# Projections of a decoder step on Trainium2: loads and TensorE's work in a written order from the fifth weight step on

## The chip, the core and the metric

The kernel runs on one core of one Trainium2 chip. A core has a matrix engine (TensorE: PE for the products, PEld for the loads of its stationary operand), three engines for elementwise work (VectorE: DVE, ScalarE: ACT, GpSimd: POOL), and SyncE (SP), which here only issues DMAs. Each engine works through its own list of instructions in order; semaphores tie the lists together. The metric is the device time of one execution in microseconds.

## The reference, cut to what matters

One inference step of a two-layer trunk for 512 prompt rows and 8 x 8 sample rows, width 1024. Layer 0 is dilated sliding-window attention, layer 1 a state-space layer, and each is followed by a gated feed-forward net. The change is in the first part of layer 0:

```python
qkv = (h @ w_qkv).reshape(B, T, 3, N_DIL, N_HEAD_SLOTS, HEAD_DIM)
q = rope(rmsnorm(qkv[:, :, 0], q_gain), pos)
k = rope(rmsnorm(qkv[:, :, 1], k_gain), pos)
v = qkv[:, :, 2]
...
s = jnp.einsum('bqhd,bqkhd->bqhk', q_blk, kf) * (HEAD_DIM ** -0.5)
```

There are three window groups: g0 (128 keys, every row), g1 (512, every 4th) and g2 (2048, every 16th). The prompt attends to itself; the 8 samples attend to their caches of keys and values, which lie in memory.

## The kernel before

**The stages.** Projections (to about 333 us), attention (to about 442 us), then the output projection, feed-forward nets and the state-space layer, in which PE is all but always busy. The change touches the projections alone.

**Weight steps.** `w_qkv` is taken in nine chunks of 512 columns, in the order q2, k2, v2, q1, k1, q0, k0, v0, v1 (letter and group), and each chunk in four steps of 256 rows: 36 weight steps, counted here from 0 to 35 (`turn[0]` in the code). In a step a weight tile `raw` (512 KB) comes from memory by a DMA on SP, ACT rounds it to `whi`, DVE makes the rest `wlo` = raw - whi, and PE runs 28 matmuls of 128x512: for each of the four prompt tiles t = 0..3 two times three (`whi` with the rows' rounded part, `wlo` with it, `whi` with their rest), then four for the sample rows (`xsp`). `raw` has four buffers, `whi` and `wlo` two each. The sums of a chunk stand in five PSUM tiles `acc`.

**After a chunk.** ACT and DVE evict the five tiles as `a` (the sample tile t = 4 through L378) and sum squares (L577, L578); a short chain (L110 to L120) makes `rq`. `finish(t)` then rotates a tile on DVE: a product `u` (L589), a sum (L591), a scaling by `rq` (L592). `turned` transposes the tile on PE (L604), ACT copies it to `qT` or `kT`, and POOL writes new keys out. The list `late` hands out `finish`, the sample tile first, at the ends of the following chunk's steps by `LATE` and `LAST`: two at the first, then one each.

**Sample scores.** For g2, the keys of a sample are multiplied elementwise with its query on DVE. A product takes a tile of the cache `kc` and a tile of queries read from a scratch in memory (`qscr`, written by SP once q2 is rotated), 512 KB each; one multiplication (L409) and one reduction into `P` (L410). There are 32, four to a sample, and `Close2` then brings a sample's `P` onto PE, adds the new keys and DVE takes the maxima (L432). For g1 and g0, a `Score` loads cache tiles, PE transposes them (L516), ACT copies, PE makes the dots (L527, L532), DVE evicts them (L534). All cache and query tiles share six buffers `kst`; `Close2` and the dots share one PSUM tile, `Sd`.

**What sets the order.** A scheduler orders each engine's list when the program is built. `keep_in_program_order` keeps marked instructions of an engine in the order in which they were written, among themselves; the others may move. Before, PE's work is kept from `PINNED` = step 20 on; `slot()` is called after each prompt tile and after the sample rows (five to a step) and runs what `later(n, ...)` set n slots ahead. `PLAN` says in which step products and scores begin, at its end: their loads are issued there, and the DVE work is written right behind.

Of the kernel before, what the change touches and what calls it, by code (L numbers as in the profile page):

```python
# [30 lines left out]
NEG = -1e30  # L31
SCALE = HD ** -0.5
KST = 6
RV, RF = 0.0, 0.7
PINNED = 20
LATE, LAST = (2, 1, 1, 1), (2, 2, 1, 0)
PLAN = {5: (2,), 6: (2,), 7: (2,), 8: (2,), 9: (2,), 10: (2,), 11: (2,), 12: (2, 2), 13: (2,), 14: (2, 2), 15: (2,), 16: (2,), 18: (2,), 19: (2,), 20: (2,),
        21: (1, 2), 22: (1, 2), 23: (1, 2), 24: (1, 2), 25: (1, 2), 26: (1, 2), 27: (1, 2), 28: (1, 2), 29: (0, 2), 30: (0, 2), 31: (0, 2),
        32: (0, 0, 2, 2), 33: (0, 2), 34: (0, 0, 2)}


def dram(ap, off, dims):
    return bass.AP(tensor=ap.tensor, offset=ap.offset + off, ap=[list(d) for d in dims])
# [286 lines left out]
                self.roots()  # L330


def qkv_chunk(nc, A, L, x, part, gi, step=None, rate=0.0, pre=None, slot=None):
    acc = L["acc"]
    c0 = (part * 3 + gi) * 512

    def mm(*a, **kw):
        ins = nc.tensor.matmul(*a, **kw)  # L338
        return ins if slot is None else L["tc"].keep_in_program_order(ins)

    ps = [acc.tile([128, 512], F32, name="acc") for _ in range(5)]
    for kk in range(4):
        raw = x.w[kk] if c0 == 1024 else L["fetch_w"](A["w_qkv"], 4608, kk * 2, 2, c0, 512, rate)
        if pre is not None and kk == 0:
            with L["tc"].issue_after(x.gmc.ins):
                wh, wl = L["split_w"](raw)
        elif pre is not None:
            with L["tc"].issue_after(x.mark[kk - 1].ins):
                wh, wl = L["split_w"](raw)
            x.lo = L["mark"][0]  # L350
# [19 lines left out]
        if step is not None:  # L370
            step()
    return ps


# [19 lines left out]
UNITS = (1, 4, 8)  # L394


def cache_tile(nc, A, pool_, name, gi, b, c0, n, kv):
    t = pool_.tile([128, 2, 512], F32, name=name)[:, :n]
    st = STRIDE[gi]
    nc.sync.dma_start(t, dram(A[CACHES[gi]], (b * WIN[gi] + c0) * 1024 + kv * 512, [[st * 1024, 128], [1024, n], [1, 512]]))  # L400
    return t


def products(nc, A, L, eng, kst, P, b, part):
    c0 = 2 * part
    kc = cache_tile(nc, A, kst, "kc", 2, b, c0, 2, 0)
    qb = kst.tile([128, 2, 512], F32, name="kc")
    nc.sync.dma_start(qb, dram(L["qscr"], (b * 8 + c0) * 512, [[0, 128], [512, 2], [1, 512]]))
    eng.tensor_tensor(kc, kc, qb, OP.mult)  # L409
    eng.tensor_reduce(P[:, :, 0:2, c0:c0 + 2].rearrange("p a h c -> p c a h"), kc.rearrange("p c (a h d) -> p c a h d", a=4, h=2), AX.X, OP.add)  # L410


class Close2:
# [9 lines left out]
    def turn(self, kept=True):  # L423
        nc, L, b = self.nc, self.L, self.b
        pin, kT, q0 = L["tc"].keep_in_program_order if kept else (lambda x: x), L["kT"][2], T + b * 8
        Sd = self.psp.tile([128, 136], F32, name=self.nm)
        ins = nc.tensor.transpose(Sd[:, 0:128], self.P.rearrange("p a b c -> p (a b c)"), L["ident"])
        pin(ins)
        for hp in range(4):
            pin(nc.tensor.matmul(Sd[hp * 32:hp * 32 + 32, 128:136], self.Q[:, hp, :], kT[:, hp, q0:q0 + 8], start=True, stop=True,  # L430
                                 tile_position=(0, hp * 32), skip_group_check=True))
        nc.vector.tensor_tensor_reduce(L["Sall"][:, b, 2, :], Sd, L["md"][:, 2, :], 1.0, -3e38, OP.add, OP.max, L["mx3"][:, b, 2:3])  # L432


def qkv_phase(nc, tc, A, es, L):
# [44 lines left out]
            queue.remove(x_)  # L480
            x_[1]()

    def score2(b, part):
        if part == 0:
            prods[b] = dk.tile([128, 4, 4, 8], F32, name="P2")
            g.memset(prods[b], 0.0)
        products(nc, A, L, v, kst, prods[b], b, part)
        if part == 3:
            c = Close2(nc, L, dk, psd, "Sd", prods.pop(b), b)
            if turn[0] < PINNED:  # L490
                c.turn(False)
            else:
                later(8, c.turn)

    class Score:
        def __init__(self, gi, b):
            self.gi, self.b, self.n = gi, b, UNITS[gi]
# [12 lines left out]
            self.kc = [cache_tile(nc, A, kst, "kc", gi, b, c0, min(2, n - c0), 0) for c0 in range(0, n, 2)]  # L510
            self.ks = {}

        def turn(self, u):
# [21 lines left out]

    fill = [[], [], []]
    turn = [0]
    zero = [0]

    def step():  # L540
        for _ in range((LATE if turn[0] < 28 else LAST)[turn[0] % 4]):
            if late:
                late.pop(0)()
        zero[0] = 0
        for gi in PLAN.get(turn[0], ()):
            x_ = fill[gi].pop(0)
            if gi == 2:
                score2(*x_)
                continue
            c = Score(gi, x_)  # L550
            if gi == 1:
                for u in range(4):
                    later(u + 3, lambda c=c, u=u: c.turn(u))
                    if u % 2:
                        later(u + 4, lambda c=c, u=u: c.dots((u - 1, u)))
            else:
                later(zero[0] + 2, lambda c=c: c.turn(0))
                later(zero[0] + 4, lambda c=c: c.dots((0,)))
                zero[0] += 1
        turn[0] += 1  # L560

    late = []

    def qk_chunk(gi, part):
        ps = qkv_chunk(nc, A, L, x, part, gi, step, 0.0, x.prep if gi == 2 and part == 0 else None, slot if turn[0] >= PINNED else None)
        sh = wk.tile([128, 5, 8], F32, name="sh")
        v.memset(sh[64:128, 4], 1.0)
        at = []
# [14 lines left out]
        def finish(t):  # L583
# [8 lines left out]
            v.tensor_tensor(a3[:pp], a3[:pp], rq[:pp, t, :, None].to_broadcast([pp, 8, 64]), OP.mult)  # L592
            if t == 4 and part == (gi < 2):
                fill[gi] += range(NB) if gi < 2 else [(b, p) for b in range(NB) for p in range(4)]
            if turn[0] < PINNED:
                turned(t, a, pp)
            else:
                later(4, lambda: turned(t, a, pp))

        def turned(t, a, pp):  # L600
            dst = (qT, kT)[part][gi]
            pt = ptp.tile([128, 4, 128], F32, name="pt")
            for hp in range(4):
                ins = te.transpose(pt[:, hp, :pp], a[:pp, hp * 128:(hp + 1) * 128], ident[:pp, :pp])  # L604
                if turn[0] >= PINNED:
                    tc.keep_in_program_order(ins)
            if gi == 0 and part == 1 and t < 4:
                s.activation(dst[:, :, t:T:4], pt, AF.Copy)
            else:
                s.activation(dst[:, :, t * 128:t * 128 + pp], pt[:, :, :pp], AF.Copy)  # L610
            if part == 1:
                kv_out(nc, A, gi, 0, t, a)
            elif gi == 2 and t == 4:
                nc.sync.dma_start(qscr, a[:64])

        late.extend((lambda t=t: finish(t)) for t in (4, 0, 1, 2, 3))

    def v_chunk(gi, wk, vt=None):
        ps = qkv_chunk(nc, A, L, x, 2, gi, step, RV, None, slot if turn[0] >= PINNED else None)
# [12 lines left out]
    qk_chunk(2, 0)  # L632
    qk_chunk(2, 1)
    v_chunk(2, wk, vt2)
    for gi in (1, 0):
        qk_chunk(gi, 0)
        qk_chunk(gi, 1)
    v_chunk(0, wk)
# [6 lines left out]
    nc.sync.dma_start(vt0, L["vtscr"].rearrange("t p c -> p t c"))  # L645
    nc.sync.dma_start(mp, A["c_mp"])
# [4 lines left out]
    assert not any(fill)  # L651
    return [vt0, vt1, vt2], mp


# [814 lines left out]
```

## Time and profile before

| what | value |
|---|---|
| median of 3 runs | 1537.76 us (1534.53 to 1542.42) |
| the profiled execution's own time | 1540.19 us |
| its span, first to last instruction | 1538.4 us |
| mean granted TensorE clock | 0.987 |
| PE busy | 1485.8 us, 97% of the span |
| DVE, ACT, POOL busy | 902.7, 521.2, 321.3 us |
| moved by DMA | 322.63 MB, mean 210 GB/s |

A row of a timeline holds the start in us from the span's beginning, the duration in us, engine, line, operation, what it writes and reads, and a count; in brackets, how long the engine stood idle before it and what ended that. SPq is the issue of a DMA on SP. A row of groups holds, after the bar, busy time in us and the mean duration in ns, then idle time before them and what ended it. A row of waits holds total, number and longest. A row of DMA issues holds the count, the size of one, and the median us to landing. A 389 ns matmul overlaps the next one, so PE's rate is read from start to start.

### The profile page before, as it was taken

The numbers are of one execution on the slowest core, as the hardware profiler recorded it, in microseconds if no ns is written. First come the engines' busy times: TensorE is split into PE (matmuls) and PEld (weight loads), VectorE is DVE, ScalarE is ACT, GpSimd is POOL, SyncE is SP. The second block draws the span as 40 slices with busy tenths as digits, with TensorE's granted clock in tenths as the row PEclk, the third lists the DMA queues.
The fourth block names the chain that finished last, engine by engine and source line by source line (L and its number), as shares of the span: only waits on it lengthen the run. The fifth ranks groups of instructions, "written<-read, shape, count | busy, mean of one in ns | idle before, by whom it ended". The sixth has DMA issues, their size and how long they took to land. (4 is left out here: it accounts for less than half of the span.)

```text
span 1538.4 us, 29552 instructions
## 1 busy us (share of the span) xinstructions
PE 1485.8 (97%) x12406; PEld 1391.0 (90%) x12406; DVE 902.7 (59%) x1507; ACT 521.2 (34%) x790; POOL 321.3 (21%) x368
## 2 busy tenths in 40 slices
PE   9999897898999999999999999999999999999998
PEld 7778675666799999999999999999999999999998
DVE  5899776444556954488789567853543333333342
ACT  4533444445544221222222353532332212221222
POOL 2012231220012107554344330030110001000100
PEclk9999999899999999999999999999999999999999
DMA  7599466788965655778766947965556555442222
GB/s 258 189 347 324 124 223 208 221 293 299 313 185 192 219 198 192 246 262 285 246 226 212 328 138 220 292 198 172 192 191 217 191 190 190 148 147 83 83 68 77
DMA packets 190493, 322.63 MB, mean 210 GB/s; under 512 B 39480, under 2 KB 137016, under 8 KB 188824
## 3 DMA queue, kind: packets, MB, share of 16 engines
q1 hardware_dynamic: 182888, 303.76, 58.9%
q10 hardware_dynamic: 4992, 10.04, 1.9%
q0 software_dynamic: 2480, 6.95, 1.2%
q8 instruction: 97, 1.59, 0.4%
q14 instruction: 36, 0.29, 0.1%
HBM read 289.22 MB, written 118.78 MB: 265 GB/s over the span
## 5 line engine op out<-in xcount | busy, mean ns | idle before, releaser
L101 DVE TENSOR_TENSOR wlo<-raw,whi 128x1024 fp32r<-128x1024 f32 x200 | 247.7, 1238 | 251.7 <-ACT whi L100 248.2
L100 ACT ACTIVATE whi<-raw 128x1024 fp32r<-128x1024 f32 x200 | 208.1, 1042 | 526.3 <-PE acc L107 407.6
L107 PE MATMUL acc<-xgl,whi 128*128 128x288 f32 x1760 | 379.0, 296 | 1.0 <-DVE xgl L172 1.0
L107 PE MATMUL acc<-xgh,wlo 128*128 128x288 f32 x1760 | 377.3, 295 | 0.0
L107 PE MATMUL acc<-xgh,whi 128*128 128x288 f32 x1760 | 377.1, 296 | 0.1
L107 PEld LDWEIGHTS acc<-xgl,whi 128*128 128x128 f32 x1760 | 282.6, 188 | 2.5 <-DVE xgl L172 1.3
L107 PEld LDWEIGHTS acc<-xgh,wlo 128*128 128x128 f32 x1760 | 282.9, 188 | 0.8 <-DVE wlo L101 0.4
L107 PEld LDWEIGHTS acc<-xgh,whi 128*128 128x128 f32 x1760 | 281.5, 188 | 0.7 <-DVE gt L906 0.3
L908 POOL TENSOR_TENSOR gt<-gt,rstd 128x576 f32<-128x576 f32 x44 | 77.2, 1756 | 430.4 <-ACT gt L907 430.3
L107 PE MATMUL acc<-hh,whi 128*128 128x288 f32 x704 | 151.3, 296 | 0.0
L107 PE MATMUL acc<-hh,wlo 128*128 128x288 f32 x704 | 151.1, 295 | 0.0
L107 PE MATMUL acc<-hl,whi 128*128 128x288 f32 x704 | 150.9, 295 | 0.0
L338 PE MATMUL acc<-wlo,xh 128*128 128x512 f32 x288 | 114.5, 399 | 2.8 <-DVE wlo L101 2.8
L338 PE MATMUL acc<-whi,xh 128*128 128x512 f32 x288 | 113.4, 415 | 1.3 <-ACT xh L277 1.1
L107 PEld LDWEIGHTS acc<-hh,wlo 128*128 128x128 f32 x704 | 113.0, 188 | 0.2 <-issue 0.2
L107 PEld LDWEIGHTS acc<-hl,whi 128*128 128x128 f32 x704 | 112.9, 188 | 0.2 <-issue 0.2
L107 PEld LDWEIGHTS acc<-hh,whi 128*128 128x128 f32 x704 | 113.0, 188 | 0.0
L338 PE MATMUL acc<-whi,xl 128*128 128x512 f32 x288 | 112.6, 398 | 0.0
L192 POOL TENSOR_TENSOR ssum<-ssum,sq 128x576 f32<-128x576 f32 x21 | 35.8, 1703 | 235.9 <-ACT sq L191 235.9
L338 PEld LDWEIGHTS acc<-wlo,xh 128*128 128x128 f32 x288 | 55.6, 193 | 14.5 <-DVE wlo L101 4.3
L338 PEld LDWEIGHTS acc<-whi,xh 128*128 128x128 f32 x288 | 55.2, 193 | 12.9 <-ACT xh L277 1.7
L409 DVE TENSOR_TENSOR kc<-kc 128x1024 f32<-128x1024 f32 x32 | 39.0, 1219 | 45.9 <-DMA kc<-qscr 45.9
(361 smaller groups left out, 1951.5 us busy)
## 6 DMA issues: line engine op xcount, KB each, us to landing
o_kv_s<-cache_kv_w SPq DMA_DIRECT2D x64, 1020.0 KB, 7.3
kc<-cache_kv_w SPq DMA_DIRECT2D x96, 512.0 KB, 5.8
raw<-ffn_w_gate SPq DMA_DIRECT2D x44, 512.0 KB, 4.1
raw<-ffn_w_up SPq DMA_DIRECT2D x44, 512.0 KB, 3.8
raw<-ffn_w_down SPq DMA_DIRECT2D x40, 512.0 KB, 3.5
raw<-w_qkv SPq DMA_DIRECT2D x36, 512.0 KB, 5.5
kc<-qscr SPq DMA_DIRECT2D x32, 512.0 KB, 6.1
o_kv_s<-cache_kv_w SPq DMA_DIRECT2D x16, 1008.0 KB, 6.1
```

Source lines behind the costliest of these rows:

```text
L100: s.activation(hi, raw, AF.Copy)
L101: mark[0] = v.tensor_tensor(lo, raw, hi.bitcast(F32), OP.subtract)
L107: te.matmul(ps[:, c, :HN], w, x[:, c * HN:(c + 1) * HN], start=first and i == 0, stop=last and i == 2)
L192: g.tensor_tensor(self.ss, self.ss, sq, OP.add)
L338: ins = nc.tensor.matmul(*a, **kw)
L409: eng.tensor_tensor(kc, kc, qb, OP.mult)
L908: g.tensor_tensor(t, t, nin.r, OP.mult)
```

## The change

- The loads of `w_qkv` from step 4 on are kept in written order on SP; step j issues the one for step j + 2.
- PE's matmuls and transposes are kept in written order from step 4 on, not 20. Transposes of a finished tile always come four slots after its `finish`; `Close2` comes ten slots after its last product was written.
- A product's two loads are issued at the beginning of the step before (`PAIRS`), in kept order; its DVE work is written behind the step's `wlo`. DVE's own order is left to the scheduler. The numbers per step change: two each in steps 12 to 15, none in 16, two in 32.
- Cache tiles of the scores (`SCORES`) are loaded at the beginning of their step, in kept order.
- `qscr` is written by a DMA of POOL, straight after the rotation, not by SP behind the transposes. The loads of `vt0` and `mp` are issued in step 34.

What is computed, and with how many instructions, stays. The core of the diff (the tables, whose rows only place the work, are cut):

```diff
-PINNED = 20
+CHUNKS = ((0, 2), (1, 2), (2, 2), (0, 1), (1, 1), (0, 0), (1, 0), (2, 0), (2, 1))
-PLAN = {5: (2,), 6: (2,), ...
+PAIRS = {6: 1, 7: 1, 8: 1, ...
+SCORES = {21: (1,), 22: (1,), ...
...
     for kk in range(4):
-        raw = x.w[kk] if c0 == 1024 else L["fetch_w"](A["w_qkv"], 4608, kk * 2, 2, c0, 512, rate)
+        mult = begin()
+        raw = raws.pop(0)
...
             wh, wl = L["split_w"](raw)
+        mult()
...
+    def begin():
+        j = turn[0]
+        if 4 <= j + 2 < 36:
+            part, gi = CHUNKS[(j + 2) // 4]
+            raw = L["ring"].tile([128, 2, 512], F32, name="raw", bufs=4)
+            kept(nc.sync.dma_start(raw, dram(A["w_qkv"], ...)))
+            raws.append(raw)
+        due = [ready.pop(0) for _ in range(PAIRS.get(j, 0))]
+        for _ in range(PAIRS.get(j + 1, 0)):
+            b, part = fill[2].pop(0)
+            kc = cache_tile(nc, A, kst, "kc", 2, b, 2 * part, 2, 0, kept)
+            qb = kst.tile([128, 2, 512], F32, name="kc")
+            kept(nc.sync.dma_start(qb, dram(qscr, ...)))
+            ready.append((b, part, kc, qb))
+        for gi in SCORES.get(j, ()):
+            b, n = fill[gi].pop(0), UNITS[gi]
+            cached.append((gi, b, [cache_tile(nc, A, kst, "kc", gi, b, c0, min(2, n - c0), 0, kept) for c0 in range(0, n, 2)]))
+        if j in notes:
+            notes[j]()
+
+        def mult():
+            for b, part, kc, qb in due:
...
+                v.tensor_tensor(kc, kc, qb, OP.mult)
+                v.tensor_reduce(prods[b][...], kc.rearrange(...), AX.X, OP.add)
+                if part == 3:
+                    later(10, Close2(nc, L, dk, psd, "Sd", prods.pop(b), b).turn)
...
-            if turn[0] < PINNED:
-                turned(t, a, pp)
-            else:
-                later(4, lambda: turned(t, a, pp))
+            if (gi, part, t) == (2, 0, 4):
+                g.dma_start(qscr, a[:64])
+            later(4, lambda: turned(t, a, pp))
...
-                ins = te.transpose(pt[:, hp, :pp], a[:pp, hp * 128:(hp + 1) * 128], ident[:pp, :pp])
-                if turn[0] >= PINNED:
-                    tc.keep_in_program_order(ins)
+                kept(te.transpose(pt[:, hp, :pp], a[:pp, hp * 128:(hp + 1) * 128], ident[:pp, :pp]))
...
-            elif gi == 2 and t == 4:
-                nc.sync.dma_start(qscr, a[:64])
```

**PE, where the sample tile and the first prompt tile of k2 are transposed.** Before, on PE; `whi_1046` and `wlo_1047` are the weights of step 13, `whi_1086` those of step 14, `a_716` and `a_696` the two tiles:

```order
L338 MATMUL acc_984<-whi_1046,xsp_121 128x512
L338 MATMUL acc_984<-wlo_1047,xsp_121 128x512
L604 MATMUL pt_776<-ident_63,a_716 128x64 x4
L604 MATMUL pt_787<-ident_63,a_696 128x128 x4
L338 MATMUL acc_980<-whi_1086,xh_119 128x512
```

And changed; `whi_794` and `wlo_795` are the weights of step 9, `whi_856` those of step 10, `a_712` and `a_692` the same two tiles:

```order
L337 MATMUL acc_732<-wlo_795,xh_119 128x512
L337 MATMUL acc_732<-whi_794,xl_120 128x512
L614 MATMUL pt_828<-ident_63,a_712 128x64 x4
L614 MATMUL pt_835<-ident_63,a_692 128x128 x4
L337 MATMUL acc_733<-whi_794,xsp_121 128x512
L337 MATMUL acc_733<-wlo_795,xsp_121 128x512
L337 MATMUL acc_733<-whi_794,xsp_121 128x512
L337 MATMUL acc_733<-wlo_795,xsp_121 128x512
L337 MATMUL acc_729<-whi_856,xh_119 128x512
```

The transposes moved from the end of step 13 to the fourth slot of step 9, ahead of that step's sample matmuls. Those of q1 moved in the same way from step 20 to step 17; those of k1 stand in step 21 in both.

**DVE, from step 10's `wlo` to the scaling of k2's sample tile.** Before, on DVE; the weights of steps 10, 11 and 12 are `raw_864`, `raw_915` and `raw_985`, and `a_716` is scaled 13 rows below the last row here:

```order
L101 TENSOR_TENSOR wlo_867<-raw_864,whi_866 128x1024
L409 TENSOR_TENSOR kc_909<-kc_909,kc_911 128x1024
L410 TENSOR_REDUCE P2_856<-kc_858 128x2x4x2
L101 TENSOR_TENSOR wlo_918<-raw_915,whi_917 128x1024
L589 TENSOR_TENSOR u_783<-a_696,C1_168 128x1024
...
L410 TENSOR_REDUCE P2_856<-kc_960 128x2x4x2
L101 TENSOR_TENSOR wlo_988<-raw_985,whi_987 128x1024
```

And changed, with seven rows left out (four short ones of the chain to `rq`, a memset, and two sums of L602); `raw_734` is the weight tile of step 10, and that of step 11 comes eight rows behind the last row here:

```order
L101 TENSOR_TENSOR wlo_857<-raw_734,whi_856 128x1024
L110 RECIPROCAL rq_719<-sq_720 128x40
L503 TENSOR_REDUCE P2_860<-kc_790 128x2x4x2
L600 TENSOR_TENSOR u_784<-a_692,C1_168 128x1024
...
L502 TENSOR_TENSOR kc_852<-kc_852,kc_854 128x1024
...
L503 TENSOR_REDUCE P2_860<-kc_852 128x2x4x2
...
L502 TENSOR_TENSOR kc_912<-kc_912,kc_914 128x1024
L600 TENSOR_TENSOR u_846<-a_697,C1_168 128x1024
...
L503 TENSOR_REDUCE P2_860<-kc_912 128x2x4x2
L502 TENSOR_TENSOR kc_916<-kc_916,kc_918 128x1024
...
L503 TENSOR_REDUCE P2_860<-kc_916 128x2x4x2
L600 TENSOR_TENSOR u_906<-a_702,C1_168 128x1024
L603 TENSOR_TENSOR a_712<-a_712,rq_719 64x512
```

The weights of steps 11 and 12, which stood between the products, moved behind the scaling; three multiplications and four reductions of the products, and three `u`, stand between step 10's `wlo` and the scaling. The like stretch of step 17 (q1, from step 18's `wlo`) has two multiplications and two reductions, that of step 21 (k1, from step 22's) one and one, that of step 5 (q2, from step 6's) none.

**SP, around the first scores.** Before, on SP; `raw` is a weight tile (`raw_1606` of step 22), `kc` a tile of a cache, or of queries where `qscr` is read:

```order
L88 DMA raw_1606<-w_qkv 128x2x512
L88 DMA raw_1699<-w_qkv 128x2x512
L400 DMA kc_1693<-cache_kv_w2048 128x2x512
L408 DMA kc_1695<-qscr_91 128x1024
L88 DMA raw_1860<-w_qkv 128x2x512
```

And changed, from the beginning of step 22 (`raw_1620` is the weight tile of step 24) to that of step 23:

```order
L482 DMA raw_1620<-w_qkv 128x2x512
L400 DMA kc_1622<-cache_kv_w2048 128x2x512
L489 DMA kc_1624<-qscr_91 128x1024
L400 DMA kc_1626<-cache_kv_w512 128x2x512
L400 DMA kc_1628<-cache_kv_w512 128x2x512
L482 DMA raw_1717<-w_qkv 128x2x512
```

Weight tiles no longer run ahead of the products' tiles as their buffers allow; each step has its weight tile first, then the pair of the next step, then its score's.

More of the change, by code (lines that the diff above doesn't have):

```diff
@@ L330, in prep, with qkv_chunk @@
                 self.roots()
-def qkv_chunk(nc, A, L, x, part, gi, step=None, rate=0.0, pre=None, slot=None):
+def qkv_chunk(nc, L, x, raws, begin, step, pre=None, slot=None):
     acc = L["acc"]
-    c0 = (part * 3 + gi) * 512
     def mm(*a, **kw):
@@ L369, in qkv_chunk @@
             slot()
-        if step is not None:
-            step()
+        step()
     return ps
@@ L394, with cache_tile @@
 UNITS = (1, 4, 8)
-def cache_tile(nc, A, pool_, name, gi, b, c0, n, kv):
+def cache_tile(nc, A, pool_, name, gi, b, c0, n, kv, kept=lambda x: x):
     t = pool_.tile([128, 2, 512], F32, name=name)[:, :n]
     st = STRIDE[gi]
-    nc.sync.dma_start(t, dram(A[CACHES[gi]], (b * WIN[gi] + c0) * 1024 + kv * 512, [[st * 1024, 128], [1024, n], [1, 512]]))
+    kept(nc.sync.dma_start(t, dram(A[CACHES[gi]], (b * WIN[gi] + c0) * 1024 + kv * 512, [[st * 1024, 128], [1024, n], [1, 512]])))
     return t
[L404 to L410, printed above, removed]
 class Close2:
@@ L481, in slot @@
             x_[1]()
[L483 to L489, printed above, removed]
-            if turn[0] < PINNED:
-                c.turn(False)
-            else:
-                later(8, c.turn)
+    kept = tc.keep_in_program_order
+    raws, ready, cached = list(x.w), [], []
@@ new lines, in begin @@
+    def begin():
[3 more added lines that the diff above has]
+            raw = L["ring"].tile([128, 2, 512], F32, name="raw", bufs=4)
+            kept(nc.sync.dma_start(raw, dram(A["w_qkv"], (j + 2) % 4 * 256 * 4608 + (part * 3 + gi) * 512, [[4608, 128], [128 * 4608, 2], [1, 512]])))
+            raws.append(raw)
[4 more added lines that the diff above has]
+            qb = kst.tile([128, 2, 512], F32, name="kc")
+            kept(nc.sync.dma_start(qb, dram(qscr, (b * 8 + 2 * part) * 512, [[0, 128], [512, 2], [1, 512]])))
+            ready.append((b, part, kc, qb))
[6 more added lines that the diff above has]
+            for b, part, kc, qb in due:
+                if part == 0:
+                    prods[b] = dk.tile([128, 4, 4, 8], F32, name="P2")
+                    g.memset(prods[b], 0.0)
+                v.tensor_tensor(kc, kc, qb, OP.mult)
+                v.tensor_reduce(prods[b][:, :, 0:2, 2 * part:2 * part + 2].rearrange("p a h c -> p c a h"), kc.rearrange("p c (a h d) -> p c a h d", a=4, h=2),
+                                AX.X, OP.add)
+                if part == 3:
+                    later(10, Close2(nc, L, dk, psd, "Sd", prods.pop(b), b).turn)
+        return mult
@@ L537, in qkv_phase @@
     turn = [0]
-    zero = [0]
+    notes = {}
     def step():
@@ L543, in step @@
                 late.pop(0)()
[L544 to L551, printed above, removed]
+        zero = 0
+        while cached:
+            c = Score(*cached.pop(0))
+            if c.gi == 1:
                 for u in range(4):
@@ L556, in step @@
             else:
-                later(zero[0] + 2, lambda c=c: c.turn(0))
-                later(zero[0] + 4, lambda c=c: c.dots((0,)))
-                zero[0] += 1
+                later(zero + 2, lambda c=c: c.turn(0))
+                later(zero + 4, lambda c=c: c.dots((0,)))
+                zero += 1
         turn[0] += 1
@@ L564, in qk_chunk @@
     def qk_chunk(gi, part):
-        ps = qkv_chunk(nc, A, L, x, part, gi, step, 0.0, x.prep if gi == 2 and part == 0 else None, slot if turn[0] >= PINNED else None)
+        first = (part, gi) == CHUNKS[0]
+        ps = qkv_chunk(nc, L, x, raws, begin, step, x.prep if first else None, None if first else slot)
         sh = wk.tile([128, 5, 8], F32, name="sh")
@@ L612, in turned @@
                 kv_out(nc, A, gi, 0, t, a)
-            elif gi == 2 and t == 4:
-                nc.sync.dma_start(qscr, a[:64])
         late.extend((lambda t=t: finish(t)) for t in (4, 0, 1, 2, 3))
     def v_chunk(gi, wk, vt=None):
-        ps = qkv_chunk(nc, A, L, x, 2, gi, step, RV, None, slot if turn[0] >= PINNED else None)
+        ps = qkv_chunk(nc, L, x, raws, begin, step, None, slot)
         for t in range(5):
@@ L630, in v_chunk @@
             kv_out(nc, A, gi, 1, t, a)
[L632 to L638, printed above, removed]
+    for part, gi in CHUNKS[:8]:
+        if part < 2:
+            qk_chunk(gi, part)
+        else:
+            v_chunk(gi, wk, vt2 if gi == 2 else None)
     assert not late
@@ L644, in qkv_phase, with values @@
     mp = vp.tile([128, 4, 512], BF16, name="mp")
-    nc.sync.dma_start(vt0, L["vtscr"].rearrange("t p c -> p t c"))
-    nc.sync.dma_start(mp, A["c_mp"])
+    def values():
+        nc.sync.dma_start(vt0, L["vtscr"].rearrange("t p c -> p t c"))
+        nc.sync.dma_start(mp, A["c_mp"])
+    notes[34] = values
     with ExitStack() as e4:
@@ L650, in qkv_phase @@
             slot()
-    assert not any(fill)
+    assert not any(fill) and not ready and not raws
     return [vt0, vt1, vt2], mp
```

19 lines of the change are left out of this document (8 added, 11 removed).

## The prediction

> **What bounds the kernel now.** I count the weight steps 0 to 35; step 4 is the fifth. First the windows by stage, for TensorE's (PE) idle time:
>
> ```profile
> 40.00:180.00 140.00, 131.04 (x613) 104.14 (x612) 130.20 (x176) 56.09 (x85) 27.41 (x45) 0.98 0.74 253
> 180.00:333.50 153.50, 137.25 (x1078) 106.34 (x1076) 86.62 (x133) 64.14 (x98) 35.85 (x95) 0.94 0.69 227
> 442.00:1538.40 1096.40, 1081.07 (x8440) 1071.80 (x8438) 610.93 (x934) 326.00 (x418) 245.55 (x203) 1.00 0.57 192
> ```
>
> After the first column pair come PE, weight loads, DVE, ACT, POOL, clock, DMA. The projections end near 333.5. PE idles 9.0 us from 40 to 180 and 16.2 us from 180 to there. DVE is busy 130.2 of 140 us in the first stretch: there it is nearly a second bound. What follows the projections keeps its work, so I carry the difference to the end one to one. PE's waits up to 345 us name the causes:
>
> ```profile
> PE Sd L427 <- DVE mx L534: 10.1, 3, 8.4
> PE acc L338 <- DVE a L378: 5.3, 1, 5.3
> PE pt L604 <- DVE a L592: 5.1, 4, 2.6
> PE acc L338 <- DVE wlo L101: 2.8, 4, 1.6
> ```
>
> All of them are for DVE. The two long ones, on DVE's and PE's timelines:
>
> ```profile
> 263.88 1.23 DVE L409 TENSOR_TENSOR kc<-kc 128x1024 f32<-128x1024 f32 x1 [3.15 <-DMA kc<-qscr]
> 267.96 0.29 DVE L534 CUSTOM_DVE_ANT_0 Sall<-Sd,md 128x136 f32<-128x136 f32 x1
> 301.06 1.23 DVE L409 TENSOR_TENSOR kc<-kc 128x1024 f32<-128x1024 f32 x1 [7.13 <-DMA kc<-qscr]
> 304.46 0.73 DVE L378 SCALAR_TENSOR_TENSOR a<-acc,rr,ks 64x512 f32<-64x512 f32 x1
> 305.34 0.76 PE L338 MATMUL acc<-whi,xsp 128*128 128x512 f32 x1 [5.29 <-DVE a L378]
> ```
>
> A product's multiplication stands in DVE's order and waits 3.15 and 7.13 us for its query tile; the eviction that PE needs is behind it. Finally the clock, in windows cut around the half-speed stretches:
>
> ```profile
> 166.70:170.10 3.40, 3.40 (x9) 2.66 (x9) 3.35 (x7) 1.63 (x3) 0.00 (x0) 0.50 0.00 0
> 176.90:180.30 3.40, 3.40 (x12) 2.72 (x11) 3.04 (x5) 1.65 (x2) 1.52 (x3) 0.50 0.60 215
> 268.30:272.50 4.20, 4.19 (x19) 2.95 (x19) 4.17 (x7) 0.60 (x1) 3.93 (x7) 0.50 0.67 183
> 305.40:310.00 4.60, 4.60 (x11) 3.63 (x12) 1.24 (x3) 1.06 (x1) 1.76 (x5) 0.50 0.96 294
> ```
>
> Each follows one of the waits. Busy at half speed for 15.6 us costs 7.8 us. So the whole prize is 9.0 + 16.2 + 7.8 = 33.0 us.
>
> **The weight loads in written order: nothing.**
>
> ```profile
> L100 ACT ACTIVATE whi<-raw 128x1024 fp32r<-128x1024 f32 x34 | 35.7, 1057 | 64.8 <-PE acc L338 59.5 <-DVE P L410 5.1
> raw<-w_qkv SPq DMA_DIRECT2D x36, 512.0 KB, 5.5
> DVE kc L409 <- DMA kc<-qscr: 45.9, 18, 7.1
> 312.32 0.38 SPq L645 DMA_DIRECT2D vt<-vtscr  x1
> ```
>
> ACT's rounding of a weight tile waits for PE, which still reads the tile two steps back (two buffers), and not for a landing. Weights are there already; earlier or tidier loads bring nothing. If that cover went, each late load would cost up to its 5.5 us to landing (second row) in that step. The loads of vt0 and mp, now tied to step 34, were issued at 312.3 before, about a step earlier and 21 us ahead of their use after 333.5: nothing either. The third row, DVE's 45.9 us for query tiles, is what the step's delay of the products is after; its part on PE's path is in the 33.0.
>
> **Products a step later, TensorE kept from step 4: removed, up to 33.0 us.** I credit all of it: the 8.4 and 5.3 lose their late tile, and what PE waited for before 180 (5.1 and 2.8) is priced anew below.
>
> **Added: pinned transposes of q2, k2, q1, k1.** A finished tile's transposes now stand four slots after its rotation was issued: steps 5, 9, 17 and 21 for the first two tiles of a chunk. Before, the scheduler set those of k2 in step 13 and of q1 in step 20. Only k1's, in step 21, were pinned there already, and this gives the price:
>
> ```profile
> 167.07 1.04 ACT L100 ACTIVATE whi<-raw 128x1024 fp32r<-128x1024 f32 x1
> 168.49 1.21 DVE L101 TENSOR_TENSOR wlo<-raw,whi 128x1024 fp32r<-128x1024 f32 x1
> 169.62 0.39 DVE L110 RECIPROCAL rq<-sq 128x40 f32<-128x40 f32 x1
> 175.21 1.88 DVE L592 TENSOR_TENSOR a<-a,rq 64x512 f32<-64x512 f32 x3
> 173.83 0.39 PE L338 MATMUL acc<-whi,xl 128*128 128x512 f32 x1
> 176.03 0.43 PE L604 MATMUL pt<-ident,a 64*128 64x64 f32 x4 [1.82 <-DVE a L592]
> ```
>
> PE ends step 20 at about 167; ACT may then round the weights of step 22, DVE subtracts, and DVE's order goes on from the reciprocal to the first L592 of three: 175.21 + 0.6 - 169.62 = 6.2 us. In the changed order the same list stands behind the same subtraction, with products set into it. Their prices, start to start:
>
> ```profile
> 73.32 1.22 DVE L410 TENSOR_REDUCE P<-kc 128x16 f32<-128x1024 f32 x1
> 74.45 1.21 DVE L409 TENSOR_TENSOR kc<-kc 128x1024 f32<-128x1024 f32 x1
> 75.58 0.68 DVE L578 TENSOR_REDUCE sh<-t 128x8 f32<-128x512 f32 x1
> 41.28 0.40 PE L338 MATMUL acc<-whi,xh 128*128 128x512 f32 x1
> 41.51 0.39 PE L338 MATMUL acc<-wlo,xh 128*128 128x512 f32 x1
> ```
>
> 1.13 us for a multiplication or a reduction; 0.23 us for a matmul, so PE is at its fourth slot after 24 x 0.23 = 5.5 us. From the step's start DVE needs at least 1.04 (rounding) + 1.13 (subtraction, 168.49 to 169.62) + 6.2 + 1.13 n, n being the products' instructions in the list. PE therefore waits at least 2.9 + 1.13 n. The orders give n = 0 in step 5, 7 in step 9 (three multiplications, four reductions), 4 in step 17 and 2 in step 21: 2.9 + 10.8 + 7.4 + 5.2 = 26.3 us. As a check on the trace, n = 0 gives 2.9 for step 21 as it was; PE came 1.7 us late through half clock, so 1.2, and it waited 1.8. Later pinned transposes (steps 25, 29) are where they were, and cost nothing after 180.
>
> Behind the waiting transposes stand the rest of the step and so the release of the weight buffers, which ACT and DVE wait for: the stall moves the whole chain, and no other engine makes it up, since DVE's own order holds the cause.
>
> **DVE's lateness on top: 8 us, bounds 0 and 12.** The queries' write to memory moves from SP to POOL's queue:
>
> ```profile
> 58.95 0.50 SPq L614 DMA_DIRECT2D qscr<-a  x1
> 61.56 0.34 SPq L408 DMA_DIRECT2D kc<-qscr  x1
> DMA to landing us min/median/max: 5.7/6.0/8.2
> ```
>
> From SP it was readable after 2.6 us; POOL's like write (to vscr, the third row; min, median, max) lands after 6.0. On POOL only set-up work stands ahead of it. That makes the first product some 3.4 us later, in a stretch where DVE has 10 us of idle time in 140, and the weight tiles of steps 8 and 9 stand behind it. The other 5 us are for DVE still at work when its weight tile is ready (above, it began 0.4 us late): about 1 us each in steps 5, 8, 9, 17, 21. If DVE's idle time takes it all in, 0; if the products' loads run late too, 12. [...]
>
> **Half clock after the four waits: 7.6 us, bounds 6.8 and 9.2.** By the four clock rows each costs 1.7 to 2.3 us.
>
> [...]
>
> **Close2 and dots in one slot: 6 us, bounds 1 and 10.** At the ends of steps 23 and 27 the closing matmuls now come due in the slot of a score's first dots, Close2 first, and both use the one PSUM tile Sd. PE waits for its eviction (0.29 us by the 267.96 row, with the handover 0.5). In DVE's order it stands behind a product whose tile comes free only as the score two steps back is turned. No trace shows it; I take 2 us each with some half clock, nearer the 1.82 than the 8.4.
>
> **Sum.** Added 26.3 + 8 + 7.6 + 6 = 47.9, less 33.0: +14.9 us. With all low bounds 34.1 - 33.0 = +1.1; with the high ones 57.5, and 6 us of the short waits left, +30.5. The profiled execution took 1540.19 us (span 1538.4), the runs' median is 1537.76, so about 1552 us as a median.
>
> **Rivals.**
> No change that can be measured (about 0.5%, 7.7 us): low bounds all round, 1539 us. For it: DVE has idle time later on; against: the chain leaves PE no slack in four places. 0.27.
> Faster: DVE clears the finish before PE gets there. It decides at 8.4 us from the step's start to the first L592; if the products in the list cost nothing there (n = 0), added is 4 x 2.9 + 6.8 + 1 = 19.4, net -13.6: 1524 us. For it: step 21 as it was; against: seven product instructions in DVE's order, which it can't pass. 0.10.
> SP's written order as a new bound: a load that waits for one of the six tiles holds the ones behind it, and the score tiles of steps 21 to 28 come late, say 2 us a step (a third of a 6.1 us load): 16 us more, 1568 us. For it:
>
> ```profile
> kc<-qscr SPq DMA_DIRECT2D x32, 512.0 KB, 6.1
> SPq L400 <- DMA kc<-qscr: 56.0, 13, 7.9
> ```
>
> SP waits much already; against: weights go first in each step, two steps ahead. 0.11.
> The change not doing what it says applies to the weight loads alone: they were early before.
>
> **Numbers.** The forecast itself (1546 to 1562) 0.52. Slower by over 0.5%: 0.52 + 0.11 = 0.63; within 0.27; faster 0.10. The range, 1533 to 1568, reaches over the low bounds and to the high ones.
>
> **What would show it.** Step 22 begins here before:
>
> ```profile
> 178.98 0.63 PE L338 MATMUL acc<-whi,xh 128*128 128x512 f32 x1
> ```
>
> PE's waits should name the transposes on L614 with DVE's a on L603: some 11 us or more in step 9, 7 in step 17, 5 in step 21; clock rows of 0.50 behind them. DVE's wait for query tiles should fall far below 45.9, and the 8.4 and 5.3 be gone. PE should reach step 22 near 205 to 212, and win back some 12 to 20 us by the end. If step 9's wait is under 3 us the forecast falls; if ACT's rounding waits for raw tiles, SP's rival stands.

## The result, and the profile after

The changed kernel takes 1554.73 us (median of 4 runs, 1553.58 to 1558.26) against 1536.14 us (1533.10 to 1542.42, 4 runs) of the kernel before: a ratio of 1.0125, 95% interval 1.0104 to 1.0145. It is slower, by 18.6 us, where 1552 was forecast. The profiled execution took 1555.63 us, its span 1553.9. Three single executions far from all others (2059 us of the kernel before, and 2898 and 2199 us in the experiments with the products behind the scaling and with later transposes) are left out of the medians here and below.

First where the time went. The windows are cut at the start of step 22 (179.0 us before, 205.7 after) and at the end of the projections (333.1 and 348.0); after the first column pair come PE, weight loads, DVE, ACT, POOL, clock, DMA. The kernel before:

```profile
40.00:179.00 139.00, 130.04 (x611) 103.33 (x610) 129.53 (x175) 55.24 (x85) 26.91 (x45) 0.98 0.74 252
179.00:333.10 154.10, 137.90 (x1068) 106.88 (x1070) 87.29 (x134) 64.59 (x99) 36.36 (x96) 0.94 0.69 227
333.10:1538.40 1205.30, 1181.09 (x10554) 1150.33 (x10552) 663.08 (x1136) 382.59 (x581) 249.40 (x207) 0.99 0.60 201
```

and the changed one:

```profile
40.00:205.70 165.70, 133.92 (x609) 108.07 (x610) 138.08 (x181) 56.74 (x84) 18.86 (x46) 0.89 0.66 234
205.70:348.00 142.30, 135.10 (x1077) 106.06 (x1079) 80.60 (x130) 64.63 (x99) 33.62 (x96) 0.97 0.66 228
348.00:1553.90 1205.90, 1182.56 (x10545) 1152.62 (x10545) 659.70 (x1134) 382.46 (x581) 250.33 (x208) 0.99 0.59 200
```

The first stretch is 26.7 us longer, the second 11.8 shorter, the third 0.6 longer: 15.5 in all. PE's idle time tells why. In the first stretch it grows from 9.0 us to 165.70 - 133.92 = 31.8, and the granted clock falls from 0.98 to 0.89. In the second it shrinks from 16.2 us to 7.2. What follows the projections keeps its time.

PE's waits up to 345 us in the changed kernel:

```profile
PE pt L614 <- DVE a L603: 26.2, 3, 11.6
PE Sd L541 <- DVE mx L423: 7.2, 2, 6.6
PE pt L614 <- issue: 3.3, 1, 3.3
PE acc L337 <- DVE a L378: 2.3, 2, 1.8
```

The first and the third row are the pinned transposes of steps 9, 17, 21 and of step 5. For step 5 the profile names nothing that ended the wait; on DVE's timeline the first scaling there starts at 56.56 and takes some 0.6 us, and PE goes on at 57.34. On PE's timeline, in that order of steps 5, 9, 17, 21 (the bracket is the idle time ahead of the row):

```profile
57.34 1.06 PE L614 MATMUL pt<-ident,a 64*128 64x64 f32 x5 [3.27 <-issue]
99.58 1.14 PE L614 MATMUL pt<-ident,a 64*128 64x64 f32 x5 [11.59 <-DVE a L603]
164.78 1.51 PE L614 MATMUL pt<-ident,a 64*128 64x64 f32 x7 [8.14 <-DVE a L603]
202.38 0.68 PE L614 MATMUL pt<-ident,a 64*128 64x64 f32 x4 [6.47 <-DVE a L603]
```

29.5 us in four places: nearly all of the first stretch's 31.8. And this is what DVE did meanwhile in step 9, from the weight subtraction to the scaling that the transposes need:

```profile
84.28 1.21 DVE L101 TENSOR_TENSOR wlo<-raw,whi 128x1024 fp32r<-128x1024 f32 x1
85.42 0.38 DVE L110 RECIPROCAL rq<-sq 128x40 f32<-128x40 f32 x1
85.73 1.15 DVE L503 TENSOR_REDUCE P<-kc 128x16 f32<-128x1024 f32 x1
...
96.59 1.21 DVE L503 TENSOR_REDUCE P<-kc 128x16 f32<-128x1024 f32 x1
97.72 1.21 DVE L600 TENSOR_TENSOR u<-a,C 128x1024 f32<-128x1024 f32 x1
98.85 1.88 DVE L603 TENSOR_TENSOR a<-a,rq 64x512 f32<-64x512 f32 x3
```

The list from the reciprocal to the end of the first scaling takes 98.85 + 0.6 - 85.42 = 14.0 us without a gap; 7 of its instructions are products. Behind each of the four waits, and behind the one of 6.57 us at the end of step 27, the clock is halved:

```profile
56.50:63.30 6.80, 5.96 (x19) 4.89 (x20) 6.21 (x9) 2.04 (x3) 2.07 (x3) 0.50 0.36 95
90.60:104.30 13.70, 4.71 (x16) 3.88 (x17) 13.70 (x19) 2.04 (x3) 1.75 (x3) 0.50 0.64 228
158.90:169.10 10.20, 4.32 (x15) 3.62 (x16) 9.75 (x15) 2.04 (x3) 3.12 (x6) 0.50 0.02 6
199.80:206.70 6.90, 4.32 (x15) 3.58 (x16) 6.83 (x12) 2.04 (x3) 2.27 (x4) 0.51 0.72 251
271.50:278.40 6.90, 4.78 (x28) 3.74 (x29) 6.35 (x11) 1.79 (x3) 0.00 (x0) 0.51 0.86 301
```

PE works 5.96 + 4.71 + 4.32 + 4.32 = 19.3 us at half speed behind the four waits, which costs 9.7 us, and 4.78 behind the fifth, which costs 2.4.

### The profile page after: what moved, and what is told of

The parts are those of the page before. It is cut to its first block, busy times and chain, and to the rows that moved or that the text cites. A ratio compares the mean times of both kernels' runs of the same rounds, so it can differ in the third digit from the quotient of the medians.

```text
span 1553.9 us, 29538 instructions
## 1 busy us (share of the span) xinstructions
PE 1488.2 (96%) x12406; PEld 1396.9 (90%) x12406; DVE 900.6 (58%) x1507; ACT 523.0 (34%) x790; POOL 311.2 (20%) x369
## 4 chain that ended last, share of the span: by engine, by line
PE 52%; DVE 2%; DMA 1%; ACT 0%; issue 0%; ACTq 0%; DVEq 0%
PE acc L107 48%; PE aux L107 1%; DMA u_scr<-uP 1%; PE acc L1261 1%; DVE cb L1171 1%; DVE kk L1180 0%; PE acc L1299 0%; PE acc L1300 0%; PE aux L1164 0%; PE aux L1300 0%; PE aux L1299 0%; PE aux L1175 0%; PE aux L937 0%; DVE Z L1281 0%; PE aux L1181 0%
## 5 line engine op out<-in xcount | busy, mean ns | idle before, releaser
L337 PE MATMUL acc<-whi,xh 128*128 128x512 f32 x288 | 118.5, 413 | 1.7 <-ACT xh L277 1.5
L337 PEld LDWEIGHTS acc<-whi,xl 128*128 128x128 f32 x288 | 55.0, 191 | 12.2
```

## Experiments

Three theories stood against each other. **A**: the transposes' places in PE's kept order cost, through DVE's list ahead of them. **B**: the products' delay and SP's written order cost. **C**: DVE simply has too much work, and whatever wait is taken away, another for DVE takes its place. Times are medians; before is measured beside them (1536.2 to 1536.8 us).

**One half of the change alone: TensorE kept from step 4.** On the kernel before:

```diff
-PINNED = 20
+PINNED = 4
```

> The kernel before with one number changed: TensorE's order is kept from step 4 in place of step 20; loads and products are as before. Theory A (the pinned transposes): DVE's list between the weight subtraction and the first scaled tile holds 0, 7, 2 and 0 product instructions in steps 5, 9, 17 and 21, so by 2.9 + 1.13 n PE waits 2.9 + 10.8 + 5.2 + 2.9 = 21.8 us, with some 7 us of half clock; against that stand about 9 us of idle time before 180 and 3.4 us of half clock that the kernel before has there. Step 22 starts at 192 to 202 (before 179.0), time 1550 to 1560. Theory B (the products' delay and SP's written order are what costs): nothing changes here, 1533 to 1542, step 22 near 179. Theory C (DVE's amount of work is the bound): work is the same as before, so within 5 us of 1537.

Measured: 1555.47 us (1553.47 to 1559.42), ratio 1.0133 (1.0105 to 1.0161). This one number costs as much as the whole change: 19.3 us. PE's two long waits of it:

```profile
103.21 1.14 PE L604 MATMUL pt<-ident,a 64*128 64x64 f32 x5 [15.13 <-DVE a L592]
169.58 1.73 PE L604 MATMUL pt<-ident,a 64*128 64x64 f32 x8 [8.77 <-DVE a L592]
```

They are longer than the 10.8 and 5.2 us that the formula gave, the one in step 21 shorter (0.9 against 2.9); step 22 starts at 203.0, just past A's 202. A stands, but its formula holds only where DVE comes to the whole list in time. Step 9 begins at 82.47 here and DVE's weight subtraction at 86.43, 4.0 us later, where the formula has 1.04; in step 21 the reciprocal (192.88) is done ahead of the subtraction (194.94), so that part of the list is no longer behind it. B is out as the only cause, and C too, since DVE's work is that of the kernel before.

**The other half: the change with TensorE kept only from step 20.**

```diff
+PINNED = 20
-    ps = qkv_chunk(nc, L, x, raws, begin, step, ..., None if first else slot)
+    ps = qkv_chunk(nc, L, x, raws, begin, step, ..., slot if turn[0] >= PINNED else None)
-            later(4, lambda: turned(t, a, pp))
+            if turn[0] < PINNED:
+                turned(t, a, pp)
+            else:
+                later(4, lambda: turned(t, a, pp))
```

(and the pins of the transposes and closing matmuls likewise)

> The changed kernel with TensorE's order kept only from step 20, as it was before; loads, the products' delay and the closing matmuls' ten slots stay. Theory A: the waits for the scaled tiles in steps 5, 9 and 17 (3.3, 11.6 and 8.1 us) and the half clock behind them (about 7.5 us) go; step 22 starts at 177 to 188, time 1525 to 1538. Theory B: the time stays at 1548 to 1557, step 22 at 200 or later, with waits for products or their tiles in place of the transposes. Theory C: DVE has 139 us of work ahead of step 22, so something of the gain stays out: step 22 at 188 to 196, 1538 to 1547.

Measured: 1530.14 us (1526.57 to 1534.83), ratio 0.9969 (0.9951 to 0.9987): faster than the kernel before by 6.0 us, and than the changed one by 24.6. Step 22 starts at 181.9. The delay and the loads are not what costs: B falls. C has this much right: at the seam of step 20, where the order begins to be kept, PE still waits for what DVE has left undone, as the timelines of PE and DVE show.

```profile
160.00 1.08 PE L622 MATMUL pt<-ident,a 128*128 128x128 f32 x4 [6.88 <-ACT t L378]
165.85 0.45 PE L622 MATMUL pt<-ident,a 128*128 128x128 f32 x1 [4.76 <-DVE a L608]
159.18 0.67 DVE L608 TENSOR_TENSOR a<-a,rq 128x512 f32<-128x512 f32 x1
```

The first row names ACT, but what PE turns there is a scaled tile, and DVE's scaling ended at 159.85, 0.15 us ahead of it.

**The dose: no products in DVE's list.** PE's order stays exactly as changed; a product's multiplication may only be issued behind the scaling of a chunk's first two tiles, which makes n = 0 in steps 9, 17 and 21 where it was 7, 4 and 2.

```diff
-                v.tensor_tensor(kc, kc, qb, OP.mult)
+                with tc.issue_after(scaled[0]):
+                    v.tensor_tensor(kc, kc, qb, OP.mult)
...
-            v.tensor_tensor(a3[:pp], a3[:pp], rq[:pp, t, :, None]...)
+            fs = v.tensor_tensor(a3[:pp], a3[:pp], rq[:pp, t, :, None]...)
+            if t in (4, 0):
+                scaled[:] = [fs.ins]
```

> The changed kernel with one rule more: a product's multiplication is issued on DVE behind the last written scaling of a chunk's first two tiles, so n is 0 in steps 5, 9, 17 and 21; PE's order and the transposes' places are untouched. Theory A: by 2.9 + 1.13 n each of the four waits is about 2.9 (together 11 to 14 us in place of 29.5), step 22 at 183 to 193, time 1530 to 1541. Theory B: the waits are for late products; pushing them back further costs, 1555 or more. Theory C: DVE's work is what is late; the 18 us come back as waits of PE for weight subtractions (a line L101) and the time is 1547 to 1556.

Measured: 1532.77 us (9 executions; interval of the ratio to before 0.9967 to 1.0002), 22.0 us under the changed kernel. The waits of steps 5, 9, 17 and 21:

```profile
57.66 0.43 PE L617 MATMUL pt<-ident,a 64*128 64x64 f32 x4 [3.29 <-issue]
88.77 0.46 PE L617 MATMUL pt<-ident,a 64*128 64x64 f32 x4 [1.39 <-DVE a L604]
145.06 1.15 PE L617 MATMUL pt<-ident,a 64*128 64x64 f32 x7 [1.19 <-DVE a L604]
175.38 0.46 PE L617 MATMUL pt<-ident,a 64*128 64x64 f32 x4 [1.69 <-DVE a L604]
```

Step 5, which had no products in its list, is as it was; the other three fall from 26.2 to 4.3 us. The only new rule is one on DVE's order, so the products in the list are shown to be the price. The 1.2 to 1.7 us are less than the 2.9 of the formula: without the products DVE does the reciprocal and the first product `u` of a rotation (in step 9 at 81.32 and 81.63) before it comes to the weight subtraction (83.06), and the whole of the list no longer stands behind it.

**The same cure from PE's side: transposes later.** PE's order is kept from step 4, DVE is left alone; the transposes come 5 or 10 slots later.

```diff
+WAITS = {(0, 2, 4): 9, (0, 2, 0): 9, (1, 2, 4): 14, (1, 2, 0): 14, ..., (0, 1, 4): 14, (0, 1, 0): 14, ...}
-            later(4, lambda: turned(t, a, pp))
+            later(WAITS.get((part, gi, t), 4), lambda: turned(t, a, pp))
-                    later(10, Close2(...).turn)
+                    later(16 if turn[0] < 12 else 10, Close2(...).turn)
```

> The changed kernel with PE's kept transposes moved back: those of q2 and k2 and of q1 and k1 by 5 or 10 slots for the first two tiles and 5 for some of the others, and the closing matmuls before step 12 by 6. PE's order is kept as before. Theory A: no PE wait for a scaled tile over 3 us in steps 5 to 21; 29.5 us of waiting and up to 9.6 us of half clock go, step 22 at 172 to 186, time 1518 to 1535. Theory B: the place of the transposes does not matter, 1548 to 1557. Theory C: PE waits for the weight subtractions instead (their own list now holds the products), step 22 at 190 or later, 1540 to 1550.

Measured: 1528.47 us (9 executions), ratio 0.9957 (0.9939 to 0.9975); step 22 starts at 181.3, and PE's waits for scaled tiles shrink to

```profile
PE pt L615 <- DVE a L604: 10.0, 4, 3.9
```

One of them is over the 3 us that A allowed; the time is in A's range and below C's.

**The weight loads alone**, on the kernel before:

```diff
-        raw = x.w[kk] if c0 == 1024 else L["fetch_w"](A["w_qkv"], ...)
+        ahead()      # kept load of the tile two steps on
+        raw = x.w.pop(0)
```

> The kernel before with its weight loads alone in a written order, two steps ahead; products and TensorE's order as before. If they cost and bring nothing, as the prediction had it: 1531 to 1541. If a good part of the 6 us by which the changed kernel with TensorE kept from step 20 beat the kernel before comes from these loads and not from the products' delay: 1528 to 1532. If SP's written order holds other loads up: over 1541.

Measured: 1536.35 us against 1536.81, ratio 0.9991 (0.9968 to 1.0013). Nothing beyond the interval, as priced.

**The shared slot.** The change set ten slots for the closing matmuls; the kernel before had eight (from step 20 on), and this run goes back to them.

```diff
-                    later(10, Close2(nc, L, dk, psd, "Sd", prods.pop(b), b).turn)
+                    later(8, Close2(nc, L, dk, psd, "Sd", prods.pop(b), b).turn)
```

> The changed kernel with the closing matmuls eight slots after the last product in place of ten, so that no score's first dots share their slot. If the shared slot is what costs: the waits of 6.6 and 0.6 us for the eviction of Sd and some 2.7 us of half clock go, 1543 to 1549; the prediction's own figure for this term was 6, so 1549. If DVE's wait for a query tile ahead of that eviction is what costs, wherever the closing matmuls stand: the wait moves to the closing matmuls themselves, 1552 to 1558.

Measured: 1548.48 us (ratio to before 1.0068, 1.0048 to 1.0088), 6.25 us under the changed kernel. DVE shows how. In the changed kernel at the end of step 27:

```profile
269.59 1.23 DVE L502 TENSOR_TENSOR kc<-kc 128x1024 f32<-128x1024 f32 x1 [6.56 <-DMA kc<-qscr]
270.85 1.22 DVE L503 TENSOR_REDUCE P<-kc 128x16 f32<-128x1024 f32 x1
271.99 1.27 DVE L589 TENSOR_REDUCE sh<-t 128x8 f32<-128x512 f32 x2
273.18 0.29 DVE L423 CUSTOM_DVE_ANT_0 Sall<-Sd,md 128x136 f32<-128x136 f32 x1
```

and with the closing matmuls two slots earlier:

```profile
263.82 0.30 DVE L423 CUSTOM_DVE_ANT_0 Sall<-Sd,md 128x136 f32<-128x136 f32 x1 [0.45 <-PE Sd L421]
269.53 1.23 DVE L502 TENSOR_TENSOR kc<-kc 128x1024 f32<-128x1024 f32 x1 [5.41 <-DMA kc<-qscr]
```

DVE waits for its tile all the same, 5.41 us in place of 6.56. But the eviction of Sd (L423) now stands ahead of that wait and not behind it, and of PE's 7.2 us for `Sd` 0.6 are left.

**The queries' write back on SP's queue.**

```diff
-                g.dma_start(qscr, a[:64])
+                nc.sync.dma_start(qscr, a[:64])
```

> The changed kernel with the queries written to memory from SP's queue again in place of POOL's. By the prediction's step the first product comes some 3.4 us earlier and up to that much is won: 1551 to 1555. If the 30.3 us that SP's queue stood behind that write in the changed kernel delay the weight tiles of steps 8 and 9 and with them the wait in step 9: 1543 to 1549. If neither is on PE's path: 1553 to 1557.

Measured: 1554.57 us (5 runs; ratio to before 1.0099, 1.0066 to 1.0132), the changed kernel's 1554.73 again. SP's queue stands still in both, in the changed kernel 30.3 us for the first product's read of the queries and here 35.5 us for the write itself. The changed kernel's row:

```profile
SPq L489 <- DMA qscr<-a: 30.3, 1, 30.3
```

Nothing that PE needs is late for it there: of ACT's waits for weight tiles in the changed kernel up to 360 us, two are for a load, and both end before 12 us.

```profile
ACT whi L100 <- PE acc L337: 29.3, 13, 5.8
ACT whi L100 <- DMA raw<-w_qkv: 4.8, 2, 4.3
```

But the run does not bring the first product 3.4 us forward: it starts at 66.88 here and at 64.25 in the changed kernel, and ACT waits 2.54 us for a weight tile here (until 61.91). What the write costs is read from the rows of the changed kernel:

```profile
57.55 0.77 POOL L607 DMA_DIRECT2D qscr<-a  x1 [32.24 <-DVE a L603]
60.05 0.34 SPq L489 DMA_DIRECT2D kc<-qscr  x1
```

From POOL's issue to the first read that had waited for it are 2.5 us; from SP it was 2.6 us before (58.95 to 61.56). The 3.4 us were never there.

**All three mendings at once**, the order kept from step 4 (products behind the scaling, transposes later, closing matmuls 14 slots after the last product before step 12 and 8 from there):

> The changed kernel, TensorE's order kept from step 4 as in it, with the products behind the scaling, the transposes later by the table of the run on it (closing matmuls at fourteen slots before step 12) and the closing matmuls eight slots after the last product from there. If the pinned transposes and the shared slot are all that a kept order costs: no PE wait over 2 us before 300, 1518 to 1526. If DVE's amount of work decides once they are gone: PE waits for weight subtractions, 1527 to 1535, no better than either mending alone.

Measured: 1523.48 us (1519.22 to 1528.71, 8 runs), ratio 0.9916 (0.9887 to 0.9944): faster than both kernels. The windows up to step 22 (171.8 here) and to the end of the projections:

```profile
40.00:171.80 131.80, 124.82 (x600) 100.55 (x600) 122.61 (x165) 54.14 (x82) 18.75 (x42) 1.00 0.69 251
171.80:314.10 142.30, 137.02 (x1085) 106.31 (x1086) 94.06 (x146) 66.19 (x101) 43.01 (x99) 0.98 0.80 267
```

DVE has 122.61 us of work ahead of step 22 where the changed kernel had 138.08: what need not be done there has moved behind it, where DVE has room (94.06 of 142.30). So C was no bound at these times either. A's "no wait over 2 us" was too strict: one of 2.6 us in step 12 and one of 3.95 in step 27 are left.

**The slot without the kept order, and with the dose.** The run with TensorE kept from step 20 and the one with the products behind the scaling, each with `later(8, ...)` for the closing matmuls:

> The changed kernel with TensorE's order kept only from step 20 and the closing matmuls eight slots after the last product. If the kept order and the shared slot are separate costs that add up: the 6.1 us by which the shared slot was dear with the order kept from step 4 go here too (PE waited 5.4 and 0.7 us there, with 3.4 us of half clock behind), 1522 to 1526. If the wait for Sd only moves to another place once PE is earlier: 1528 to 1533.

> The changed kernel, order kept from step 4, transposes in their places, with the products behind the scaling and the closing matmuls eight slots after the last product. If the two costs add up: 1533.7 less about 6, 1525 to 1530, and PE's waits in steps 9, 17 and 21 stay under 2 us. If the closing matmuls' own wait (5.0 us near the end of step 30 in the run with ten slots) only moves: 1531 to 1536.

Measured: 1523.71 us (ratio 0.9921, 0.9902 to 0.9940) and 1527.12 us (0.9956, 0.9932 to 0.9980). The two slots are worth 6.4 and 5.65 us here, and 6.25 in the changed kernel: a separate cost that adds up. The 5.65 is the coarsest of the three, since the six executions of that run go from 1523.55 to 1535.17 us. In it PE waits 1.5, 1.5 and 2.1 us in steps 9, 17 and 21, the last a little over the 2 us expected, and one wait of 3.6 us for `Sd` is left.

With these runs the change can be taken apart in medians, each edit against its neighbour (before taken as 1536.4):

| edit | from | to | us |
|---|---|---|---|
| weight loads in written order | 1536.8 | 1536.4 | -0.5 |
| products a step later, cache loads in written order (with the weight loads; eight slots, TensorE from step 20) | 1536.4 | 1523.7 | -12.7 |
| TensorE kept from step 4 | 1523.7 | 1548.5 | +24.8 |
| closing matmuls at ten slots | 1548.5 | 1554.7 | +6.2 |

The first row is part of the second; the last three make +18.3, of 18.6 measured. The shares hold for this order of the edits: on the kernel before, the third alone cost 19.3 us.

## Why the prediction was right, point by point

- **The weight loads, nothing.** Right: 0.9991 of the time before, alone.
- **The prize, 33.0 us.** Nearly right in size. PE's idle time that is not one of the new waits is 31.8 - 29.5 = 2.3 us in the first stretch and 7.2 - 7.2 = 0 in the second; 30.7 went. But the way was not what the text said. It credited the delay with curing the late product tiles. DVE's wait for them "should fall far below 45.9"; it is 36.9 in the changed kernel, which is the point that failed:

```profile
DVE kc L502 <- DMA kc<-qscr: 36.9, 16, 6.6
```

Between the starts of step 22 and the end of the projections it fell from 41.1 to 21.9 us, and ahead of step 22 it rose from 4.8 to 15.1. Loads written a step ahead still stand in SP's queue behind one that waits for a free tile, here until 258.61:

```profile
258.61 1.31 SPq L400 DMA_DIRECT2D kc<-cache_kv_w  x2
259.97 0.46 SPq L482 DMA_DIRECT2D raw<-w_qkv  x1
260.52 0.42 SPq L400 DMA_DIRECT2D kc<-cache_kv_w  x1
261.04 0.49 SPq L489 DMA_DIRECT2D kc<-qscr  x1
```

The last of these is the tile that DVE came to at 263.0 and had at 269.59. The loads at 258.61 could leave when the product before had given its tile back, and that product had itself come late:

```profile
257.36 1.23 DVE L502 TENSOR_TENSOR kc<-kc 128x1024 f32<-128x1024 f32 x1 [5.50 <-DMA kc<-qscr]
```

It ends at 258.59. By the times, with six tiles each late product makes the next one's load late. So the 8.4 us of before came back as 6.57 under another name, with the eviction again behind a product that waits for its tile.
- **Four pinned transposes, 26.3 us.** Right in place, order and size: 3.27, 11.59, 8.14 and 6.47 us, 29.5 in all, against the floors 2.9, 10.8, 7.4 and 5.2. The dose shows that the products in the list carry it. Two things were off. The fixed part is not 2.9 but 0.9 to 1.7 us where DVE gets part of the list done ahead of the weight subtraction; taking the products out therefore saved more than 1.13 us for each, (11.59 - 1.39) / 7 = 1.5 us in step 9, 1.7 in step 17 and 2.4 in step 21. And DVE can come late to the list: pinning alone gave 15.1 us with seven products, where the subtraction began 4.0 us into the step.
- **DVE's lateness on top, 8 us.** Over-sized. The waits exceed their floors by 29.5 - 26.3 = 3.2 us. This is the term furthest off: the 3.4 us in it for the queries' write from POOL's queue were read from another write (to vscr, 6.0 us), and this one was there after 2.5 us, as soon as from SP (2.6).
- **Half clock after the four waits, 7.6 us.** Under-sized by 2: 9.7, above the upper bound 9.2. 3.0 of it stand behind the shortest of the four waits, the 3.27 us of step 5 (5.96 us at 0.50).
- **The shared slot, 6 us.** Right: 6.25, 6.4 and 5.65 in three settings. By the rows it was 7.2 idle and 2.4 of half clock; when it is taken away, some 3 us of that are waited elsewhere (1.75 us at a transposition in step 29, for one). The cause is the change's own move of the closing matmuls from eight slots to ten.
- **The sum.** With the measured terms, 29.5 + 9.7 + 6.2 - 30.7 = +14.7; at the end of the projections the profiled executions stand 348.0 - 333.1 = 14.9 us apart. That the forecast's +14.9 is met so closely is partly luck: lateness came out 4.8 us below its term, while half clock was 2.1 above, and 2.3 us of the prize stayed in. The medians are 18.6 us apart, 3 more than the two profiled executions (15.4), within what runs of one kernel differ by.
- **Step 22 at 205 to 212, and 12 to 20 us won back.** The first came out at 205.7; 11.8 us were won back, just under the range.
- **The rivals.** No change: fell, for the four waits are no bounds but present in full. Faster through n = 0: fell here, but names the right lever, since with n made 0 the kernel is 22 us faster (1532.77; the rival's figure was 1524, without the shared slot 1527.12). SP's order as the bound: SP's queue does stand still for 30.3 us, but ACT waits 4.8 us for raw tiles in all, both times before 12 us. What came true of it is the late product tile above, and with the eviction ahead of it PE waits 0.6 us for `Sd` in place of 7.2.

## What to carry to other kernels

An order kept on one engine cost nothing by itself here: kept from step 4 and kept from step 20 come out alike (1523.5 and 1523.7 us) once each kept instruction stands where its input is ready. Before keeping an order, count for each pinned instruction what stands ahead of its producer in the producer's own order; n instructions of 1.13 us there come back as that wait and more. And where one buffer is shared, put its release ahead of whatever on that engine may wait for a transfer; two slots were worth 6 us here in three settings.

## What the runs showed of the hardware

In these traces the length of a wait does not tell by itself whether the granted clock is halved behind it. In step 21 of the kernel before, PE waits 1.82 us, until 176.03. The 3.40 us in which this falls, columns as above:

```profile
173.50:176.90 3.40, 1.41 (x11) 0.87 (x10) 3.40 (x6) 0.39 (x1) 0.71 (x2) 1.00 0.00 0
```

PE was busy 1.41 us of them at full clock, and the next 3.40 us are at 0.50 (the row from 176.90 among the prediction's clock rows). A longer wait, of 2.77 us, in the kernel with TensorE kept from step 4 was not followed by half clock:

```profile
322.39 0.47 PE L338 MATMUL acc<-whi,xsp 128*128 128x512 f32 x1 [2.77 <-DVE a L378]
```

The windows of that kernel around it:

```profile
317.20:320.60 3.40, 2.42 (x25) 1.69 (x23) 0.24 (x1) 0.00 (x0) 0.00 (x0) 1.00 1.05 320
320.60:324.00 3.40, 1.61 (x7) 1.40 (x8) 2.98 (x5) 0.65 (x1) 1.35 (x3) 1.00 0.67 236
324.00:327.40 3.40, 3.40 (x18) 2.82 (x18) 2.50 (x3) 1.01 (x2) 0.41 (x2) 1.00 0.74 211
```

The wait falls on the first two, in which PE was busy 2.42 and 1.61 us (idle 1.0 and 1.8), and all three are at 1.00. What decides between the two cases is not shown: no run was made for it, and these rows are read from traces made for other ends.
